# A decoder trunk on one Trainium2 core: a fourth Strassen unit in the last gate pair, earlier first splits, and another bank for the last group

## The chip, the cores and the metric

The kernel runs on one core of one Trainium2 chip. The metric is the device time of one execution in microseconds (us). Before the change it was 808.76 us, the median of 3 runs that lay between 808.56 and 809.57 us.

In the text PE is the matmul engine (TensorE), DVE the vector engine, ACT the scalar engine, POOL is GpSimd, and SP is the engine whose queue issues the DMAs. Each engine works through its own instructions strictly in the order in which the built program has them.

## The reference, cut to what matters

One layer on 256 tokens of width 2048, all in float32. The branches make a merge `m`, which is multiplied by `w_o`; then comes a gated per-layer embedding and a last norm:

```python
m = jax.nn.sigmoid(ga) * (ya @ w_a_out[i]) + jax.nn.sigmoid(gb) * (yb @ w_b_out[i])
x = x + m @ w_o[i]
gate = jax.nn.sigmoid(rmsnorm(x, ple_norm_g[i]) @ w_ple_gate[i])
x = x + gate * (p[i] @ w_ple_proj[i])
...
return rmsnorm(x, final_norm_g)
```

The change lies in the product with `w_ple_gate` (2048 x 2048, called `w_pg` in the kernel) and in what stands just before and behind it.

## The kernel before, in words

**Splits.** Every float32 product is made of three fp32r matmuls: weights and operands are split into a high part and a low remainder, and hi·hi, hi·lo and lo·hi are added up in PSUM. The weights arrive in raw tiles of 1 MB (tag `raw`, three buffers), which the SP queue loads. `split` (L143 and on) makes `whi` from a raw tile on ACT (L166) and `wlo` on DVE (L167), a [128, 1024] piece at a time; such a piece is one *position* of the plan. The three matmuls of one position for one 128-token half are recorded at L1265 (plain groups) or L1287 (pairs). The tokens are two halves, t = 0 and 1.

**The plan.** `groups` lists the products one after the other, each with 512 output columns or, for a pair, with 1024. The last ones are `OO` (a pair of `w_o`), two plain `w_o` groups, then for `w_pg`: the plain group PG 0 (columns 0 to 511), the pair GP (columns 512 to 1535, the program `LATE`), and the plain group PG 3 (columns 1536 to 2047), called the last group here. PG 0 has 8 positions of 12 matmuls.

**Pairs and Strassen units.** A pair is a list of units. A unit `(g, c)` takes two weight pieces of column half `g`; `(2, c)` takes the same piece `c` of both halves. Each has 2 splits and 24 matmuls. A unit `("S", c)` makes the piece `c` of both halves in Strassen's manner, in four positions: 21 matmuls and 4 splits (one of them half as wide), but DVE must first combine the weights in place (`combine_weights`, L181, L184, L185), and the operand has to be there in combined *forms* too (`forms`, tiles `So0`, `So1`). The sums 1, 5, 6 and 7 of the Strassen units gather in PSUM banks of tag `s`, those of the four outputs in banks of tag `g`; each tag has four banks. When the counts in `left` are at zero, `sums` adds the banks up on DVE (L852), after ACT has copied the first `s` bank (L865).

**The operand.** The operand of `w_pg` is the new `x`, turned. Each `w_o` group gives a quarter of it: `ep_o` adds it to `x`, sends it through DRAM (`turned`: four DMAs out, one back), DVE transposes blocks (L355), and `put` splits it with the norm's gain into `xh` on ACT (L310) and `xl` on DVE (L311). The last quarter (columns 1536 to 2047 of `x`) is read by positions 6 and 7 of PG 0. The third argument, 4 for that quarter, says how many steps later the transposition is recorded.

**The order.** The code records instructions in a loop over positions; `ahead(pos)` says how many positions ahead the splits are recorded, and rises from 3 to 8 in the course of the pair. A scheduler then decides how they stand on each engine, bound by data and by the few `issue_after` lines; what it made is seen in the built program only.

**The gates.** `gated` takes the sums of 512 columns: ACT the sigmoid (L1021), DVE the product with the projected embedding `pw` (L1024) and the sum into `xs` (L1025), ACT the squares (L1026), POOL the product with the last norm's gain (L1033). For the last group, `last_half` does the same in pieces of 256 columns (L1041, L1042, L1045, L1049). `sums_so_far` (L1058 to L1070) and `last_norm` (L1076, L1079) make the norm's factors, half of it on POOL; L1083, L1085 and L1087 scale `x`, and six DMAs write it out.

Of the kernel before, what the change touches and what calls it, by code (L numbers as in the profile page):

```python
# [12 lines left out]
ALU = mybir.AluOpType  # L13
PSUM = bass.MemoryType.PSUM

P = 128
# [7 lines left out]
CW = 512  # L24
# [19 lines left out]
INNER = (0, 4), ("S", 0), (0, 6), ("S", 1), (2, 3), ("S", 2), (1, 4), (1, 6)  # L44
FRONT = (0, 2), (0, 4), (0, 6), ("S", 0), (1, 2), ("S", 1), (1, 4), (1, 6)
OUT = (0, 4), ("S", 0), (1, 4), ("S", 1), (2, 3), ("S", 2), (0, 6), (1, 6)
LATE = (0, 4), ("S", 0), (0, 6), ("S", 1), (2, 3), ("S", 2), (1, 4), (1, 6)


PRM_GMIX, PRM_GPLE, PRM_GHG, PRM_LB, PRM_CONV = 0, 16, 32, 40, 48  # L50
# [5 lines left out]
def hybrid_kernel(ctx, tc, xT, x, pT, prm, gfin, masks, w_in, w_a, w_b, w_o, w_pg, w_pp, out):  # L56
    nc = tc.nc
# [23 lines left out]
    state = {"tmp": "tmp1"}  # L81
# [3 lines left out]
    def nm(s):  # L85
        uid[0] += 1
        return f"{s}_{uid[0]}"

    def t4(tag="t4", bufs=None):
        bufs = bufs or {"tmp1": 8, "tmp2": 4, "tmp3": 5}[state["tmp"]]  # L90
        return pools[state["tmp"]].tile([P, 1024], F32, tag=tag, bufs=bufs, name=nm(tag))

    def bank(tag):
        return ps.tile([P, CW], F32, tag=tag, bufs=4, name=nm(tag))

    def sc(n, tag="sc", bufs=12):
        return small.tile([P, n], F32, tag=tag, bufs=bufs, name=nm(tag))
# [9 lines left out]
    def load(pos):  # L107
        if unit_of[pos] not in loaded and groups[steps[pos][0]][0] == "O":
            with tc.issue_after(state["sent"]):
                return load_raw(pos)  # L110
        return load_raw(pos)
# [62 lines left out]
    def combine_weights(pos):  # L174

        b = load(pos).rearrange("p i (k c) -> p (i k) c", k=2)
        pool, tag, n = ("tmp2", "t2", 2) if more(pos) in ("gates", "last") else ("tmp3", "t2", 1)
        if more(pos) in ("inner", "first"):
            pool, tag, n = "tmp1", ("both", "aoff")[unit_of[pos] // 2 % 2], 1
        t2 = half[unit_of[pos]] = pools[pool].tile([P, CW], F32, tag=tag, bufs=n, name=nm("t2"))  # L180
        nc.vector.tensor_tensor(  # L181
            out=b[:, 0:4:3, :], in0=b[:, 0:3:2, :], in1=b[:, 3:4, :].to_broadcast([P, 2, CW]), op=ALU.subtract
        )
        nc.vector.tensor_tensor(out=t2, in0=b[:, 2, :], in1=b[:, 0, :], op=ALU.add)  # L184
        nc.vector.tensor_tensor(out=b[:, 1, :], in0=b[:, 1, :], in1=t2, op=ALU.subtract)  # L185

# [14 lines left out]
    groups += [("OO", 0, w_o, 0, "mT", OUT), ("O", 2, w_o, 2, "mT"), ("O", 3, w_o, 3, "mT")]  # L201
    groups += [("PG", 0, w_pg, 0, "x1T"), ("GP", 1, w_pg, 1, "x1T", LATE), ("PG", 3, w_pg, 3, "x1T")]
    steps = []
# [25 lines left out]
    LEAD = 3  # L229
# [10 lines left out]
    gates, late = of_kind("GG"), of_kind("PG")[0]  # L240
# [18 lines left out]
    def more(pos):  # L259

        return "gates" if pos in gates else "last" if pos in last else "outer" if pos in outer else "first" if pos in g0 else "inner" if any(pos in at for at in inner) else None
# [24 lines left out]
    def gain(base, k):  # L286
        return prm_t[:, base + k : base + k + 1]
# [15 lines left out]
    def put(op, k, src, scale=None):  # L303

        hi, lo = op[0][:, k, :], op[1][:, k, :]
        if scale is None:
            nc.scalar.activation(out=hi, in_=src, func=AF.Copy)
            nc.vector.tensor_tensor(out=lo, in0=src, in1=hi.bitcast(F32), op=ALU.subtract)
        else:
            a = nc.scalar.activation(out=hi, in_=src, func=AF.Identity, scale=scale)  # L310
            v = nc.vector.scalar_tensor_tensor(  # L311
                out=lo, in0=src, scalar=scale, in1=hi.bitcast(F32), op0=ALU.mult, op1=ALU.subtract
            )
            return a.ins, v.ins
# [12 lines left out]
    def blocks(ap):  # L327

        return ap.rearrange("p (c b e) -> p c b e", b=4, e=32)

    def spread(ap, t):

        return ap.rearrange("p (b c t e) -> p t c b e", b=4, c=4, t=NT)[:, t]

    def turned(src, lag, dst=None):

        d = dram.tile([P, 4, T], F32, tag="turn", bufs=3, name=nm("turn"))
        to = d.rearrange("(b i) a x -> a i b x", b=4)
        for a in range(4):
            state["sent"] = nc.sync.dma_start(
                out=to[a], in_=src[32 * a : 32 * a + 32, :].rearrange("i (b x) -> i b x", b=4)
            ).ins
        yield  # L350
        nc.sync.dma_start(out=src, in_=d.rearrange("p a x -> p (a x)"))
        for _ in range(lag):
            yield
        dst = t4() if dst is None else dst
        nc.vector.transpose(  # L355
            out=dst.rearrange("p (k a e) -> p a k e", a=4, e=32), in_=src.rearrange("p (a k e) -> p a k e", a=4, e=32)
        )
        return dst
# [439 lines left out]
    def form_tiles(pool, tag, n=2):  # L798

        return lambda: tuple(pool.tile([P, 4 * n * P], F32R, tag=tag + x, bufs=1, name=nm(tag + x)) for x in "hl")  # L800
# [50 lines left out]
    def add(out, x, y):  # L851
        nc.vector.tensor_tensor(out=out, in0=x, in1=y, op=ALU.add)  # L852
# [95 lines left out]
    def ep_o(j, psum):  # L948
        xs = state["x"]
        x1 = t4()  # L950
        for t in range(NT):
            d = xs[:, t, j * CW : (j + 1) * CW]
            add(d, d, psum[t])
            nc.scalar.activation(out=spread(x1, t), in_=blocks(d), func=AF.Copy)
        turn = turned(x1, (2, 6, 6, 4)[j])
        next(turn)
        yield
        junk = t4()
        next(turn)
        for t in range(NT):  # L960
            nc.scalar.activation(
                out=junk[:, t * CW : (t + 1) * CW], in_=xs[:, t, j * CW : (j + 1) * CW], func=AF.Square,
                accum_out=state["ss2"][:, t * 4 + j : t * 4 + j + 1],
            )
        yield
        x1 = yield from turn
        if j < 2:
            for c in range(4):
                h = x1[:, c * T : (c + 1) * T]
                nc.scalar.activation(out=h, in_=h, func=AF.Identity, scale=gain(PRM_GPLE, j * 4 + c))  # L970
            hi, lo = (x[:, j * 4 : j * 4 + 4, :].rearrange("p k t -> p (k t)") for x in state["x1T"])
            nc.scalar.activation(out=hi, in_=x1, func=AF.Copy)
            nc.vector.tensor_tensor(out=lo, in0=x1, in1=hi.bitcast(F32), op=ALU.subtract)
            yield
            chunks = [c for u, c in LATE if u == "S" and c // 2 == j]
            r = x1.rearrange("p (u k t) -> p u k t", u=2, k=2)[:, : len(chunks)]
            yield from forms("x1T", form_tiles(pools["tmp3"], f"So{j}", len(chunks)), r, chunks)
            return
        for c in range(4):
            state["splits"] = put(state["x1T"], j * 4 + c, x1[:, c * T : (c + 1) * T], gain(PRM_GPLE, j * 4 + c))  # L980
        if j == 3:
            tot = sc(2, "tot2", 1)
            nc.vector.tensor_reduce(
                out=tot, in_=state["ss2"].rearrange("p (t j) -> p t j", t=NT),
                axis=mybir.AxisListType.X, op=ALU.add,
            )
            state["rstd2"] = rsqrt_of(tot, NT, D, "r2")
# [257 lines left out]
    def advance():  # L1245
        for e in list(active):
            step(e)
# [5 lines left out]
    def ahead(pos):  # L1253

        at, n = more(pos + LEAD), 0
        while n < len(MORE[at]) and more(pos + LEAD + n + 1) == at and (at == "gates" or more(pos + LEAD - 2 * n) == at):
            n += 1
        return LEAD + min(max(pos - late - 4, 0) // 3, 5) + n

    def product(psum, op, k, t, hi, lo, first, last, which=(0, 1, 2)):  # L1260

# [64 lines left out]
    for pos, (gi, c) in enumerate(steps[:last_group]):  # L1326
# [7 lines left out]
        order = ExitStack()  # L1334
# [77 lines left out]
        for i in range(2):  # L1412
            k = 2 * c + i
            for c0, c1 in EARLY[0][:2] if pos == 0 and i == 0 else ((0, CW),):
                s = slice(i * CW + c0, i * CW + c1)
# [35 lines left out]

    nlast = len(steps) - last_group
    for t, halves in ((0, (0, 1)), (1, (0,)), (1, (1,))):
        bk, n = bank("g"), CW // 2
        for c in range(nlast):
            if done < len(steps):
                split(done)
                done += 1
            hi, lo = parts[last_group + c]
            for i in range(2):  # L1460
                k = 2 * c + i
                s = slice(i * CW + halves[0] * n, i * CW + (halves[-1] + 1) * n)
                product(bk[:, : len(halves) * n], state["x1T"], k, t, hi[:, s], lo[:, s], k == 0, k == KT - 1)
            if c % 2:
                advance()
        if t == 0:
            active.append(ep_last(t, [bk[:, h * n : (h + 1) * n] for h in halves]))
        else:
            last_half(t, halves[0], bk[:, :n])
            if halves[0] == 0:  # L1470
                sums_so_far(t)
# [76 lines left out]
```

## Time and profile before

| what | value |
|---|---|
| time, median of 3 runs | 808.76 us (808.56 to 809.57) |
| profiled execution, its own time | 808.2 us |
| its span, first to last instruction | 806.4 us |
| PE busy | 797.0 us, 99% of the span |
| DVE busy | 685.2 us, 85% |
| ACT busy | 494.3 us, 61% |
| POOL busy | 94.5 us, 12% |
| mean granted PE clock | 0.998 |

The span is 1.8 us shorter than the time of the same execution. All positions in time below are in us from the span's start. In a row of the timeline stand the start, how long it took, the engine and the line, what is written and read with its shape, how many instructions of that kind follow each other ("x2"), and in brackets how long the engine had been idle before it and what released it. Tiles have their buffer numbers left out there: `t` is any of the work tiles, `g` and `s` are PSUM banks.

### The profile page before, as it was taken

What the parts mean: (1) busy time and instruction counts of PE and PEld (TensorE: products, weight loads), DVE (VectorE), ACT (ScalarE), POOL (GpSimd) and SP (SyncE); (2) the same over time, 40 slices, a digit from 0 to 9 for tenths busy, and PEclk for the clock granted to TensorE, in tenths of its full rate; (3) what the DMA queues carried; (4) which work ended last, traced back from release to release, by engine and by line L of the source; (5) the groups of instructions that cost most, each with busy time, mean ns of one, the idle gap of its engine ahead of it and who ended that gap; (6) DMA issues with size and microseconds to landing.
All of it is one profiled execution on the core that took longest, in us unless ns stands there. A gap on an engine that the chain in (4) does not pass through costs nothing. (4 is left out here: it accounts for less than half of the span.)

```text
span 806.4 us, 11109 instructions
## 1 busy us (share of the span) xinstructions
PE 797.0 (99%) x4168; PEld 662.0 (82%) x4169; DVE 685.2 (85%) x794; ACT 494.3 (61%) x666; POOL 94.5 (12%) x74
## 2 busy tenths in 40 slices
PE   9999999999999999999999999999999999999995
PEld 7888888888888888888888888888888888888785
DVE  5969797966778987978998998998998988859995
ACT  7867565575665755586674564564565557746562
POOL 0000145300000044300001001000100000002032
PEclk9999999999999999999999999999999999999999
DMA  9898855747676755667584775775875679985542
GB/s 340 309 335 313 269 175 206 234 165 240 242 262 208 259 172 196 213 217 250 189 306 158 234 274 170 235 265 179 280 267 192 207 247 360 327 299 207 201 178 104
DMA packets 50309, 191.20 MB, mean 237 GB/s; under 512 B 5712, under 2 KB 15184, under 8 KB 36304
## 3 DMA queue, kind: packets, MB, share of 16 engines
q1 hardware_dynamic: 50112, 190.24, 68.6%
q8 instruction: 32, 0.52, 0.3%
q10 hardware_dynamic: 144, 0.26, 0.1%
q14 instruction: 21, 0.17, 0.1%
HBM read 175.80 MB, written 14.68 MB: 236 GB/s over the span
## 5 line engine op out<-in xcount | busy, mean ns | idle before, releaser
L167 DVE TENSOR_TENSOR wlo<-raw,whi 128x1024 fp32r<-128x1024 f32 (+1 forms) x320 | 391.1, 1246 | 83.6 <-ACT whi L166 82.1
L166 ACT ACTIVATE whi<-raw 128x1024 fp32r<-128x1024 f32 (+1 forms) x320 | 326.2, 1047 | 163.9 <-PE g L1265 93.5
L1265 PE MATMUL g<-whi,xh 128*128 128x512 f32 (+1 forms) x464 | 177.4, 383 | 0.0
L1265 PE MATMUL g<-whi,xl 128*128 128x512 f32 (+1 forms) x464 | 177.2, 382 | 0.0
L1265 PE MATMUL g<-wlo,xh 128*128 128x512 f32 (+1 forms) x464 | 177.1, 382 | 0.0
L1287 PE MATMUL g<-wlo,xh 128*128 128x512 f32 x316 | 122.9, 389 | 0.0
L1287 PE MATMUL g<-whi,xl 128*128 128x512 f32 x316 | 122.9, 389 | 0.0
L1287 PE MATMUL g<-whi,xh 128*128 128x512 f32 x316 | 122.4, 389 | 0.0
L1265 PEld LDWEIGHTS g<-whi,xl 128*128 128x128 f32 x464 | 87.2, 188 | 17.0
L1265 PEld LDWEIGHTS g<-wlo,xh 128*128 128x128 f32 x464 | 87.2, 188 | 16.7
L1265 PEld LDWEIGHTS g<-whi,xh 128*128 128x128 f32 x464 | 87.2, 188 | 16.7
L166 ACT ACTIVATE whi<-t 128x512 fp32r<-128x512 f32 x25 | 15.8, 632 | 90.8 <-DVE t L184 90.8
L1287 PEld LDWEIGHTS g<-whi,xl 128*128 128x128 f32 x316 | 59.3, 188 | 12.4
L1287 PEld LDWEIGHTS g<-wlo,xh 128*128 128x128 f32 x316 | 59.3, 188 | 12.3
L1287 PEld LDWEIGHTS g<-whi,xh 128*128 128x128 f32 x316 | 59.3, 188 | 12.2
L934 POOL TENSOR_TENSOR t<-ga,gb 128x512 f32<-128x512 f32 x6 | 10.6, 1793 | 188.0 <-issue 118.1
L181 DVE TENSOR_TENSOR raw<-raw 128x1024 f32<-128x1024 f32 x25 | 31.6, 1263 | 0.7
L1265 PE MATMUL g<-whi,yaTh 128*128 128x512 f32 (+1 forms) x74 | 28.0, 385 | 0.0
L1265 PE MATMUL g<-wlo,yaTh 128*128 128x512 f32 (+1 forms) x74 | 27.9, 383 | 0.0
L1265 PE MATMUL g<-whi,yaTl 128*128 128x512 f32 (+1 forms) x74 | 27.9, 383 | 0.0
L1265 PE MATMUL g<-whi,ybTh 128*128 128x512 f32 x64 | 24.9, 389 | 0.0
L1265 PE MATMUL g<-wlo,ybTh 128*128 128x512 f32 x64 | 24.9, 389 | 0.0
(317 smaller groups left out, 1114.9 us busy)
## 6 DMA issues: line engine op xcount, KB each, us to landing
raw<-in_w_in SPq DMA_DIRECT2D x68, 1024.0 KB, 4.9
raw<-in_w_in SPq DMA_DIRECT2D x37, 512.0 KB, 5.1
raw<-in_w_o SPq DMA_DIRECT2D x12, 1024.0 KB, 5.9
raw<-in_w_pg SPq DMA_DIRECT2D x12, 1024.0 KB, 5.6
raw<-in_w_in SPq DMA_DIRECT2D x38, 256.0 KB, 5.1
turn<-t SPq DMA_DIRECT2D x72, 128.0 KB, 2.8
t<-turn SPq DMA_DIRECT2D x18, 512.0 KB, 4.9
raw<-in_w_a SPq DMA_DIRECT2D x8, 1024.0 KB, 5.4
```

Of the source, the lines that this page charges most:

```text
L166: a = nc.scalar.activation(out=hi[:, s], in_=src[:, s], func=AF.Copy)
L167: v = nc.vector.tensor_tensor(out=lo[:, s], in0=src[:, s], in1=hi[:, s].bitcast(F32), op=ALU.subtract)
L181: nc.vector.tensor_tensor(out=b[:, 0:4:3, :], in0=b[:, 0:3:2, :], in1=b[:, 3:4, :].to_broadcast([P, 2, CW]), op=ALU.subtract)
L934: (nc.vector if j == 3 else nc.gpsimd).tensor_tensor(out=spread(m, t), in0=blocks(ga[:, s]), in1=blocks(gb[:, s]), op=ALU.add)
L1265: nc.tensor.matmul(psum, a, b, start=first and n == 0, stop=last and n == 2)
L1287: nc.tensor.matmul(banks[name], x, y[:, s], start=k == total[name] and i == 0, stop=k == 1 and i == 2)
```

## The change

It has five edits. In `LATE`, the unit `(2, 3)` and one place of order give way to `("S", 3)`, so that four of the eight units are Strassen units, the last of them just ahead of the final plain unit. The forms of the second quarter are made for two pieces in place of one (that follows from `LATE`). `ahead` reaches its depth two positions sooner. The last quarter's transposition is recorded one step later (5 for 4), and the combination of the weights of the first Strassen unit after it has to stand behind the last `put`. The last group's first accumulation takes a bank of tag `s` in place of `g`.

```diff
-LATE = (0, 4), ("S", 0), (0, 6), ("S", 1), (2, 3), ("S", 2), (1, 4), (1, 6)
+LATE = (0, 4), ("S", 0), (0, 6), ("S", 1), (1, 4), ("S", 2), ("S", 3), (1, 6)
...
-        nc.vector.tensor_tensor(
-            out=b[:, 0:4:3, :], in0=b[:, 0:3:2, :], in1=b[:, 3:4, :].to_broadcast([P, 2, CW]), op=ALU.subtract
-        )
+        with ExitStack() as order:
+            for i in state.pop("puts", ()):
+                order.enter_context(tc.issue_after(i))
+            nc.vector.tensor_tensor(
+                out=b[:, 0:4:3, :], in0=b[:, 0:3:2, :], in1=b[:, 3:4, :].to_broadcast([P, 2, CW]), op=ALU.subtract
+            )
...
-        turn = turned(x1, (2, 6, 6, 4)[j])
+        turn = turned(x1, (2, 6, 6, 5)[j])
...
         if j == 3:
+            state["puts"] = state["splits"]
...
-        return LEAD + min(max(pos - late - 4, 0) // 3, 5) + n
+        return LEAD + min(max(pos - late - 2, 0) // 3, 5) + n
...
-        bk, n = bank("g"), CW // 2
+        bk, n = bank("g" if t else "s"), CW // 2
```

The changed file has up to four lines more, so its line numbers are higher by 3 or 4: L355 becomes L358, L1024 becomes L1028, L1265 becomes L1269, L1287 becomes L1291. What the scheduler made of it is shown at three places.

**DVE, around the last quarter's transposition.** Before, from the last split of PG 0 to the first gates (`wlo_1137` and `wlo_1140` are the splits of the pair's first unit, `wlo_1142` the first of its first Strassen unit):

```order
L167 TENSOR_TENSOR wlo_1130_6365<-raw_1113_6271,whi_1129_6364 128x1024
L983 TENSOR_REDUCE tot2_1132_6390<-ss2_1036_5822 128x2
L320 TENSOR_SCALAR r2v_1133_6392<-tot2_1132_6390 128x2
L355 STREAM_TRANSPOSE t4_1131_6380<-t4_1114_6273 128x4x8x32
L311 SCALAR_TENSOR_TENSOR xl_1039_5826<-t4_1131_6380,prm_t_84,xh_1038_5825 128x256 x4
L167 TENSOR_TENSOR wlo_1137_6399<-raw_1123_6326,whi_1136_6398 128x1024
L167 TENSOR_TENSOR wlo_1140_6417<-raw_1123_6326,whi_1139_6416 128x1024
L167 TENSOR_TENSOR wlo_1142_6433<-raw_1128_6360,whi_1141_6432 128x1024
L181 TENSOR_TENSOR raw_1128_6360<-raw_1128_6360 128x2x512
```

Now, from the same split on (`wlo_1133`, `wlo_1135` and `wlo_1142` are the same three):

```order
L167 TENSOR_TENSOR wlo_1130_6365<-raw_1113_6271,whi_1129_6364 128x1024
L167 TENSOR_TENSOR wlo_1133_6383<-raw_1123_6326,whi_1132_6382 128x1024
L167 TENSOR_TENSOR wlo_1135_6387<-raw_1123_6326,whi_1134_6386 128x1024
L987 TENSOR_REDUCE tot2_1138_6414<-ss2_1036_5822 128x2
L323 TENSOR_SCALAR r2v_1139_6416<-tot2_1138_6414 128x2
L167 TENSOR_TENSOR wlo_1142_6421<-raw_1128_6360,whi_1141_6420 128x1024
L358 STREAM_TRANSPOSE t4_1137_6404<-t4_1114_6273 128x4x8x32
L314 SCALAR_TENSOR_TENSOR xl_1039_5826<-t4_1137_6404,prm_t_84,xh_1038_5825 128x256 x4
L184 TENSOR_TENSOR raw_1128_6360<-raw_1128_6360 128x2x512
```

The three splits moved ahead of the transposition. Six rows further, the remaining split of that Strassen unit (`wlo_1150`) now stands ahead of the first gates (L1028), where before it stood behind them (L1024, L1025). The splits of the next unit stand behind the gates in both, on DVE (`wlo_1156`) as on ACT (`whi_1155`, behind the two sigmoids of L1021, now L1025).

**PE, at the seam of PG 0 and the pair.** `g_1118` and `g_1119` are the two banks of PG 0, `g_1151` to `g_1154` banks of the pair. Before, PG 0's position 6 (`whi_1126`) follows its position 5 (`whi_1124`):

```order
L1265 MATMUL g_1119_6293<-whi_1124_6328,xh_1038_5825 128x512
L1265 MATMUL g_1119_6293<-wlo_1125_6329,xh_1038_5825 128x512
L1265 MATMUL g_1119_6293<-whi_1124_6328,xl_1039_5826 128x512
L1265 MATMUL g_1118_6292<-whi_1126_6344,xh_1038_5825 128x512
L1265 MATMUL g_1118_6292<-wlo_1127_6345,xh_1038_5825 128x512
L1265 MATMUL g_1118_6292<-whi_1126_6344,xl_1039_5826 128x512
```

Now the pair's first unit stands behind position 5:

```order
L1269 MATMUL g_1119_6293<-whi_1124_6328,xh_1038_5825 128x512
L1269 MATMUL g_1119_6293<-wlo_1125_6329,xh_1038_5825 128x512
L1269 MATMUL g_1119_6293<-whi_1124_6328,xl_1039_5826 128x512
L1291 MATMUL g_1153_6478<-whi_1132_6382,xh_1038_5825 128x512
L1291 MATMUL g_1153_6478<-wlo_1133_6383,xh_1038_5825 128x512
L1291 MATMUL g_1153_6478<-whi_1132_6382,xl_1039_5826 128x512
```

and PG 0's position 6 comes 30 matmuls later, behind the first position of the Strassen unit:

```order
L1291 MATMUL g_1153_6478<-whi_1141_6420,xh_1038_5825 128x512
L1291 MATMUL s_1160_6516<-wlo_1142_6421,xh_1038_5825 128x512
L1291 MATMUL s_1160_6516<-whi_1141_6420,xl_1039_5826 128x512
L1291 MATMUL g_1153_6478<-wlo_1142_6421,xh_1038_5825 128x512
L1291 MATMUL g_1153_6478<-whi_1141_6420,xl_1039_5826 128x512
L1269 MATMUL g_1118_6292<-whi_1126_6344,xh_1038_5825 128x512
L1269 MATMUL g_1118_6292<-wlo_1127_6345,xh_1038_5825 128x512
```

So 30 matmuls of the pair (24 of the unit `(0, 4)` and 6 of the Strassen unit) moved ahead of the last 24 of PG 0.

**DVE, at the end.** Before, the first 128 tokens' sums are finished and scaled (L1085, L1087) ahead of the next piece (`t4_1232`):

```order
L1058 TENSOR_TENSOR ss3_1037_5823<-ss3_1037_5823 128x1
L1062 TENSOR_REDUCE tot3_1229_6899<-ss3_1037_5823 128x1
L1076 TENSOR_TENSOR tot3_1229_6899<-tot3_1229_6899,ss3_1037_5823 128x1
L1085 TENSOR_SCALAR xs_5814<-xs_5814,r3_1231_6907 128x256 x2
L1087 SCALAR_TENSOR_TENSOR xs_5814<-xs_5814,r3_1231_6907,gfin_t_6044 128x512
L1042 TENSOR_TENSOR t4_1232_6954<-t4_1232_6954,pw_1218_6767 128x256
```

Now the next piece (`t4_1237`) stands among those sums:

```order
L1062 TENSOR_TENSOR ss3_1037_5823<-ss3_1037_5823 128x1
L1046 TENSOR_TENSOR t4_1237_6964<-t4_1237_6964,pw_1227_6809 128x256
L1066 TENSOR_REDUCE tot3_1234_6909<-ss3_1037_5823 128x1
L1049 TENSOR_TENSOR xs_5814<-xs_5814,t4_1237_6964 128x256
L1080 TENSOR_TENSOR tot3_1234_6909<-tot3_1234_6909,ss3_1037_5823 128x1
L1053 SCALAR_TENSOR_TENSOR t4_1237_6964,ss3_1037_5823<-xs_5814 128x256
L1089 TENSOR_SCALAR xs_5814<-xs_5814,r3_1236_6917 128x256 x2
L1091 SCALAR_TENSOR_TENSOR xs_5814<-xs_5814,r3_1236_6917,gfin_t_6044 128x512
```

Three instructions of 256 columns moved ahead of the first half's scaling.

## The prediction

> **What bounds the kernel now.** First the page's busy times, then the waits of PE.
>
> ```profile
> PE 797.0 (99%) x4168; PEld 662.0 (82%) x4169; DVE 685.2 (85%) x794; ACT 494.3 (61%) x666; POOL 94.5 (12%) x74
> PE s L1287 <- DVE wlo L167: 0.2, 1, 0.2
> ```
>
> PE is busy nearly all the time, and the view of its waits names one late wait. The starts of matmuls in PE's timeline show more (the pair runs from 733.21, the last group from 775.78, its first piece of 256 columns from 786.66):
>
> ```profile
> 733.21 0.39 PE L1287 MATMUL g<-whi,xh 128*128 128x512 f32 x1
> 740.69 0.39 PE L1287 MATMUL s<-whi,So0h 128*128 128x512 f32 x1
> 741.14 0.50 PE L1287 MATMUL s<-wlo,So0h 128*128 128x512 f32 x1
> 751.52 0.40 PE L1287 MATMUL s<-whi,So0h 128*128 128x512 f32 x1
> 752.08 0.50 PE L1287 MATMUL s<-wlo,So0h 128*128 128x512 f32 x1 [0.17 <-DVE wlo L167]
> 775.78 0.39 PE L1265 MATMUL g<-whi,xh 128*128 128x512 f32 x1
> 786.66 0.28 PE L1265 MATMUL g<-whi,xh 128*128 128x256 f32 x1
> 798.05 0.28 PE L1265 MATMUL g<-whi,xl 128*128 128x256 f32 x1
> ```
>
> From 775.78 to 786.66 stand 48 matmuls: one per 0.2267 us, whatever a row says of its length. The pair has 5 x 24 + 3 x 21 = 183, which is 41.48 us, but takes 42.57. So PE loses 1.09 us there, at the first two Strassen units, each time for a `wlo`: in this stretch DVE hands over just in time. DVE's timeline there, with the first gates (L1024, L1025) in the middle:
>
> ```profile
> 720.11 0.17 DVE L320 TENSOR_SCALAR r2v<-tot 128x2 f32<-128x2 f32 x1
> 725.61 1.25 DVE L355 STREAM_TRANSPOSE t<-t 128x1024 f32<-128x1024 f32 x1 [5.34 <-DMA t<-turn]
> 729.59 3.50 DVE L167 TENSOR_TENSOR wlo<-raw,whi 128x1024 fp32r<-128x1024 f32 x3 [0.47 <-ACT whi L166]
> 737.46 1.29 DVE L1024 TENSOR_TENSOR t<-t,pw 128x512 f32<-128x512 f32 x2
> 738.66 1.29 DVE L1025 TENSOR_TENSOR xs<-xs,t 128x512 f32<-128x512 f32 x2
> 739.87 4.62 DVE L167 TENSOR_TENSOR wlo<-raw,whi 128x1024 fp32r<-128x1024 f32 x4
> 744.52 2.20 DVE L181 TENSOR_TENSOR raw<-raw 128x1024 f32<-128x1024 f32 x1
> 746.76 1.67 DVE L184 TENSOR_TENSOR t<-raw 128x512 f32<-128x512 f32 x1
> 755.47 1.23 DVE L181 TENSOR_TENSOR raw<-raw 128x1024 f32<-128x1024 f32 x1
> 756.73 0.69 DVE L184 TENSOR_TENSOR t<-raw 128x512 f32<-128x512 f32 x1
> 757.45 0.69 DVE L185 TENSOR_TENSOR raw<-raw,t 128x512 f32<-128x512 f32 x1
> 758.18 0.69 DVE L167 TENSOR_TENSOR wlo<-t,whi 128x512 fp32r<-128x512 f32 x1
> 759.35 6.90 DVE L167 TENSOR_TENSOR wlo<-raw,whi 128x1024 fp32r<-128x1024 f32 x6 [0.48 <-ACT whi L166]
> 767.70 2.36 DVE L167 TENSOR_TENSOR wlo<-raw,whi 128x1024 fp32r<-128x1024 f32 x2 [1.45 <-ACT whi L166]
> ```
>
> The reader is to see that DVE is idle for 5.34 us while the last quarter of `x` comes back from DRAM, and then has hardly a gap until 766.2.
>
> **The change part by part.**
>
> *The three splits.* They fill 3.50 us of those 5.34 us. That alone is worth little: what comes next on DVE decides.
>
> *The seam on PE.* Thirty matmuls of the pair now stand ahead of PG 0's last 24, so PG 0 ends 30 x 0.2267 = 6.80 us later: at 740.01 in place of 733.21. The first gates take PG 0's two banks, whose last matmuls stand fourth from the end and at the end: starts at 739.10 and 739.78. How soon ACT follows is shown by the last piece:
>
> ```profile
> 735.99 1.25 ACT L1021 ACTIVATE t<-g,r2r 128x512 f32<-128x512 f32 x2
> 798.37 0.47 ACT L1041 ACTIVATE t<-g,r2r 128x256 f32<-128x256 f32 x1 [3.19 <-PE g L1265]
> ```
>
> 798.37 - 798.05 = 0.32, and a sigmoid takes some 0.63. So the second one ends at 739.78 + 0.32 + 0.63 = 740.73, where before both were done at 737.24. DVE's second product starts then (0.6), the two sums follow (1.2), and the next split (`wlo_1156`) starts at 742.5. Before, it was the second of the four from 739.87, at 741.0. **DVE resumes 1.5 us later.** All that it can do ahead (puts until 729.1, a combination of 2.7 and splits of 2.9) is done at 734.7, so it idles 5 to 6 us ahead of the gates: the old gap is moved, not closed. On ACT the splits `whi_1155` and on, on DVE all further splits, are queued behind those gates, and PE waits for them.
>
> *The fourth unit.* On PE it saves 3 x 0.2267 = 0.68 us. On DVE the combination takes 758.18 - 755.47 = 2.71, three splits 3 x 6.90/6 = 3.45, the half one 0.6, together 6.8 against 2.3 for the two splits of a plain unit: **4.5 us more**. The idle time of 1.45 us at 767.70 (a raw tile's load) lies behind the third Strassen unit before and should lie behind the fourth now; I count it once in both, between 0 and another 1.45.
>
> *POOL.* L181 took 2.20 and L184 1.67 at 744.52, against 1.23 and 0.69 at 755.47. In that stretch POOL multiplied for the first gates:
>
> ```profile
> 740.82 7.06 POOL L1033 TENSOR_TENSOR xs<-xs,gfin_t 128x512 f32<-128x512 f32 x2 [19.76 <-ACT t L1026]
> 788.00 2.73 POOL L1033 TENSOR_TENSOR xs<-xs,gfin_t 128x512 f32<-128x512 f32 x2 [2.59 <-ACT t L1026]
> ```
>
> The gates and the next combination move together, so I leave the two hits of 0.97 where they are; at best they vanish (-1.95).
>
> *The second quarter's forms* for two pieces: four operations grow from 128 to 256 columns and one remainder from 512 to 1024, by the rows of such splits (0.69 and 1.15) 0.5 us and by the columns about 0.5 us more. DVE has room behind it:
>
> ```profile
> 710.08 1.22 DVE L167 TENSOR_TENSOR wlo<-raw,whi 128x1024 fp32r<-128x1024 f32 x1 [1.72 <-ACT whi L166]
> ```
>
> That covers 1.0; uncovered, it would push PG 0's splits, which PE needs only 5 us later. It costs nothing. So do the later `pw` loads on SP's queue (their readers come later still) and the new `issue_after` (the combination stands behind the puts on DVE anyway).
>
> *The end.* DVE is 1.5 + 4.5 = 6.0 us late when it finishes the last pair's gates. What follows before:
>
> ```profile
> 786.48 1.28 DVE L1025 TENSOR_TENSOR xs<-xs,t 128x512 f32<-128x512 f32 x2
> 788.93 2.08 DVE L1042 TENSOR_TENSOR t<-t,pw 128x256 f32<-128x256 f32 x2 [1.17 <-ACT t L1041]
> 790.93 0.75 DVE L1045 TENSOR_TENSOR xs<-xs,t 128x256 f32<-128x256 f32 x2
> 792.29 0.15 DVE L1058 TENSOR_TENSOR ss<-ss 128x1 f32<-128x1 f32 x1
> 792.66 0.16 DVE L1076 TENSOR_TENSOR tot<-tot,ss 128x1 f32<-128x1 f32 x1
> 793.49 0.61 DVE L1085 TENSOR_SCALAR xs<-xs,r 128x256 f32<-128x256 f32 x2 [0.66 <-POOL r L1079]
> 794.02 0.74 DVE L1087 SCALAR_TENSOR_TENSOR xs<-xs,r,gfin_t 128x512 f32<-128x512 f32 x1
> 795.22 0.42 DVE L1042 TENSOR_TENSOR t<-t,pw 128x256 f32<-128x256 f32 x1 [0.45 <-ACT t L1041]
> 796.60 0.16 DVE L1058 TENSOR_TENSOR ss<-ss 128x1 f32<-128x1 f32 x1
> 797.87 0.16 DVE L1070 TENSOR_TENSOR xs<-tot,tot 128x1 f32<-128x1 f32 x1 [0.73 <-POOL tot L1069]
> 798.88 0.43 DVE L1042 TENSOR_TENSOR t<-t,pw 128x256 f32<-128x256 f32 x1 [0.85 <-ACT t L1041]
> ```
>
> Gates done at 787.76 + 6.0 = 793.8; the first sums 792.29 - 787.76 = 4.5 later, at 798.3; five instructions in the new order (0.15, 0.33, 0.17, 0.33, 0.16) until 799.4; POOL and back 0.67, 800.1; scaling 1.27, 801.4; the second sums with their POOL step 1.43, 802.8. There the last piece's product starts, at 798.88 before: **3.9 us later**. The lateness of 6.0 has lost 2.1 in gaps that were waits for PE or ACT, and in the piece that stands among the sums. From here on to the output nothing changes.
>
> *PE beside it.* It must be done by 802.8 - 0.83 = 802.0. From 798.05 it loses 0.68, gains 1.5 at the second Strassen unit (it waited for DVE there already), and 0 to 2 at the fourth and where the last group waits for its `s` bank (ACT copies that sum behind late splits): 798.9 to 800.9. So PE is no longer what ends the kernel, and those waits cost nothing more.
>
> **Sum.** 806.4 + 3.9 = 810.3 us of span. The profiled execution took 808.2, 0.56 under the median; the same difference put on the median gives 808.76 + 3.9 = **812.7 us**.
>
> **The rivals.**
>
> *Faster: the splits pay for the unit.* Were the first gates not held by the seam, DVE would be 3.5 us ahead from the transposition on, and only 1.0 behind at the last group, where waits of 1.17, 0.45 and 0.85 absorb it; PE's 1.09 us of waits would go with the 0.68: 808.76 - 1.77 = 807.0. It decides from the point where `wlo_1156` starts: at 741.0 or earlier. For it speaks the gap of 5.34 us; against it the order on PE, which is fixed. 5%.
>
> *Only the matmuls count.* PE has 99% of the span and DVE slack elsewhere: 808.76 - 0.68 = 808.1. Against it: PE's losses at 741.14 and 752.08 are DVE's. 5%. The Trainium skill, in "Perfetto Trace Analysis", section Identifying Performance Opportunities, says that improving a kernel generally means improving its most-contended engine; by that rule this result would come. The rows of the pair's stretch speak against it.
>
> *POOL's hits miss.* If the products with the gain fall into the new gap or behind the combination, DVE gets 1.95 back: 812.7 - 1.95 = 810.7. For it: POOL's two took 2.73 at 788.00, with DVE idle. Against: they follow the squares, which follow DVE's sums, so they cannot fall into the gap. 13%.
>
> *More waits.* A raw tile late once more (1.45), or PE past 802.0: 814.2 to 814.8. 11%.
>
> **How the numbers follow.** Forecast 66%, with half a microsecond to either side for the resumption and 0.5 for the unit's price: 811.7 to 813.7. The range takes in the two neighbours: 810.4 to 814.8, and leaves out the first two rivals. Within 0.2% (1.6 us, about what a measurement of this kernel can tell from no change) lie the second rival and a third of POOL's: 9%. Faster by more: 5%. Slower by more: 86%.
>
> **What would show it.** In the changed profile DVE's wait ahead of L358 is under 2 us, and a wait of 5 to 6 us for ACT's L1025 stands ahead of L1028, at about 740. PE's L1269 rows of PG 0 end at 740. L184 and L187 of the second Strassen unit are long again. PE waits for `whi` or `wlo` there and at the fourth unit. The last matmul starts at 799 to 801, and the last L1046 over 1 us after the sigmoid ahead of it. Wrong it would be if `wlo_1156` starts before 741, or if DVE has gaps of more than 2 us behind the fourth unit.

## The result, and the profile after

The changed kernel takes **812.60 us** (median of 7 runs, 812.32 to 813.28) against 808.76 before, 3.84 us more. The ratio estimated from the runs of both is 1.0041, with a 95% interval from 1.0030 to 1.0053: slower. (That of the two medians is 1.0047. The seven runs of the kernel before beside it have the same median, 808.76, and lie between 808.27 and 811.78.) The profiled execution took 812.58 us, with a span of 810.8 us, 4.4 us above the one before.

The busy times of the page have hardly moved, and could not have told it:

```profile
PE 797.4 (98%) x4165; PEld 661.0 (82%) x4166; DVE 690.5 (85%) x799; ACT 495.7 (61%) x668; POOL 88.9 (11%) x74
```

PE has three matmuls fewer, DVE 5.3 us more. The seam is seen in PE's timeline. The last matmul of PG 0's position 5 starts at 727.65 and the pair's first unit follows; PG 0's last matmul starts at 739.89 (732.99 before):

```profile
727.65 0.39 PE L1269 MATMUL g<-whi,xl 128*128 128x512 f32 x1
727.88 0.39 PE L1291 MATMUL g<-whi,xh 128*128 128x512 f32 x1
...
739.89 0.39 PE L1269 MATMUL g<-whi,xl 128*128 128x512 f32 x1
740.12 0.62 PE L1291 MATMUL s<-whi,So0h 128*128 128x512 f32 x2
...
751.39 0.51 PE L1291 MATMUL s<-whi,So0h 128*128 128x512 f32 x1 [0.86 <-ACT whi L166]
752.34 0.50 PE L1291 MATMUL s<-whi,So0h 128*128 128x512 f32 x1 [0.45 <-ACT whi L166]
...
777.98 0.50 PE L1269 MATMUL s<-whi,xh 128*128 128x512 f32 x1 [0.70 <-ACT t L868]
...
800.42 0.28 PE L1269 MATMUL g<-whi,xl 128*128 128x256 f32 x1
```

The same on DVE, from the transposition to the end. The brackets are to be read one after the other: the gap ahead of L358 has shrunk from 5.34 to 0.55, and a new one of 5.25 stands ahead of the first gates. The old gap isn't wholly gone: 1.55 us of it now stand ahead of the third split, whose `whi` comes after a raw tile's load.

```profile
724.41 1.23 DVE L167 TENSOR_TENSOR wlo<-raw,whi 128x1024 fp32r<-128x1024 f32 x1 [1.55 <-ACT whi L166]
726.19 1.25 DVE L358 STREAM_TRANSPOSE t<-t 128x1024 f32<-128x1024 f32 x1 [0.55 <-DMA t<-turn]
...
740.41 1.33 DVE L1028 TENSOR_TENSOR t<-t,pw 128x512 f32<-128x512 f32 x2 [5.25 <-ACT t L1025]
741.65 1.29 DVE L1029 TENSOR_TENSOR xs<-xs,t 128x512 f32<-128x512 f32 x2
742.86 4.58 DVE L167 TENSOR_TENSOR wlo<-raw,whi 128x1024 fp32r<-128x1024 f32 x3
747.47 2.20 DVE L184 TENSOR_TENSOR raw<-raw 128x1024 f32<-128x1024 f32 x1
749.71 0.69 DVE L187 TENSOR_TENSOR t<-raw 128x512 f32<-128x512 f32 x1
...
776.52 2.36 DVE L167 TENSOR_TENSOR wlo<-raw,whi 128x1024 fp32r<-128x1024 f32 x2 [1.58 <-ACT whi L166]
...
793.14 1.28 DVE L1029 TENSOR_TENSOR xs<-xs,t 128x512 f32<-128x512 f32 x2
795.58 2.08 DVE L1046 TENSOR_TENSOR t<-t,pw 128x256 f32<-128x256 f32 x2 [1.17 <-ACT t L1045]
...
803.25 0.16 DVE L1074 TENSOR_TENSOR xs<-tot,tot 128x1 f32<-128x1 f32 x1 [0.73 <-POOL tot L1073]
803.33 0.42 DVE L1046 TENSOR_TENSOR t<-t,pw 128x256 f32<-128x256 f32 x1
```

DVE is 742.86 - 741.0 = 1.9 us late behind the first gates, 794.42 - 787.76 = 6.7 us late behind the last pair's, and 803.33 - 798.88 = 4.45 us late at the last product. That last row has no bracket: its sigmoid on ACT was done at 802.03 + 0.45 = 802.48, so DVE and not PE ends the kernel.

```profile
802.03 0.45 ACT L1045 ACTIVATE t<-g,r2r 128x256 f32<-128x256 f32 x1
```

### The profile page after: what moved, and what is told of

It reads as the page before. It is cut to its first block, busy times and chain, and to the rows that moved or that the text cites. A ratio compares the mean times of both kernels' runs of the same rounds, so it can differ in the third digit from the quotient of the medians.

```text
span 810.8 us, 11121 instructions
## 1 busy us (share of the span) xinstructions
PE 797.4 (98%) x4165; PEld 661.0 (82%) x4166; DVE 690.5 (85%) x799; ACT 495.7 (61%) x668; POOL 88.9 (11%) x74
## 4 chain that ended last, share of the span: by engine, by line
PE 90%; DVE 5%; issue 2%; ACT 1%; DMA 1%; POOL 0%; ACTq 0%; POOLq 0%; DVEq 0%
PE g L1269 48%; PE g L1291 29%; PE s L1291 7%; PE s L1269 3%; DVE wlo L167 2%; DMA raw<-in_w_pg 1%; PE s L514 1%; DVE raw L184 1%; DVE t L1028 1%; PE s L1142 1%; DVE xs L1029 0%; DVE t L855 0%; DVE t L1046 0%; ACT whi L166 0%; DVE t L187 0%
## 5 line engine op out<-in xcount | busy, mean ns | idle before, releaser
L1269 PE MATMUL g<-whi,xh 128*128 128x512 f32 (+1 forms) x448 | 171.2, 383 | 0.0
L1269 PE MATMUL g<-wlo,xh 128*128 128x512 f32 (+1 forms) x448 | 170.9, 382 | 0.0
L1269 PE MATMUL g<-whi,xl 128*128 128x512 f32 (+1 forms) x448 | 170.9, 382 | 0.0
L1291 PE MATMUL g<-wlo,xh 128*128 128x512 f32 x310 | 120.6, 389 | 0.0
L1291 PE MATMUL g<-whi,xl 128*128 128x512 f32 x310 | 120.6, 389 | 0.0
L1291 PE MATMUL g<-whi,xh 128*128 128x512 f32 x310 | 120.0, 389 | 0.0
L1269 PEld LDWEIGHTS g<-whi,xl 128*128 128x128 f32 x448 | 84.2, 188 | 16.4
L1269 PEld LDWEIGHTS g<-whi,xh 128*128 128x128 f32 x448 | 84.2, 188 | 16.2
L1269 PEld LDWEIGHTS g<-wlo,xh 128*128 128x128 f32 x448 | 84.2, 188 | 16.1
L1291 PEld LDWEIGHTS g<-whi,xl 128*128 128x128 f32 x310 | 58.2, 188 | 12.1
L1291 PEld LDWEIGHTS g<-wlo,xh 128*128 128x128 f32 x310 | 58.2, 188 | 12.0
L1291 PEld LDWEIGHTS g<-whi,xh 128*128 128x128 f32 x310 | 58.2, 188 | 12.0
L184 DVE TENSOR_TENSOR raw<-raw 128x1024 f32<-128x1024 f32 x26 | 32.8, 1261 | 0.7
L1269 PE MATMUL g<-whi,yaTh 128*128 128x512 f32 (+1 forms) x74 | 28.0, 385 | 0.0
L1269 PE MATMUL g<-wlo,yaTh 128*128 128x512 f32 (+1 forms) x74 | 27.9, 384 | 0.0
L1269 PE MATMUL g<-whi,yaTl 128*128 128x512 f32 (+1 forms) x74 | 27.9, 383 | 0.0
L1269 PE MATMUL g<-whi,ybTh 128*128 128x512 f32 x64 | 24.9, 389 | 0.0
L1269 PE MATMUL g<-wlo,ybTh 128*128 128x512 f32 x64 | 24.9, 389 | 0.0
```

The source lines that it names most:

```text
L184: nc.vector.tensor_tensor(out=b[:, 0:4:3, :], in0=b[:, 0:3:2, :], in1=b[:, 3:4, :].to_broadcast([P, 2, CW]), op=ALU.subtract)
L1269: nc.tensor.matmul(psum, a, b, start=first and n == 0, stop=last and n == 2)
L1291: nc.tensor.matmul(banks[name], x, y[:, s], start=k == total[name] and i == 0, stop=k == 1 and i == 2)
```

## The experiments

The theory to be tried: the 3.84 us are DVE's lateness at the end, made of the resumption behind the first gates (which the seam on PE holds back) and of the fourth unit's work, less what the tail absorbs. The rivals: the unit alone does it; the moves alone; the bank; POOL.

| kernel | seam on PE | Strassen units | median us | ratio to before, 95% |
|---|---|---|---|---|
| changed | 30 matmuls between | 4 | 812.60 | 1.0041 (1.0030 to 1.0053) |
| e1_unit | as before | 4 | 811.78 | 1.0038 (1.0024 to 1.0052) |
| e2_moves | 30 between | 3 | 810.03 | 1.0014 (1.0003 to 1.0025) |
| e3_bank | 30 between | 4 | 813.90 | 1.0059 (1.0046 to 1.0072) |
| e4_seam | 3 between | 4 | 808.89 | 0.9995 (0.9987 to 1.0004) |
| e5_three | 3 between | 3 | 807.48 | 0.9971 (0.9962 to 0.9980) |
| e6_nopool | 30 between | 4 | 810.85 | 1.0023 (1.0014 to 1.0032) |
| e7_tail | 3 between | 4 | 807.11 | 0.9973 (0.9962 to 0.9984) |
| e8_twelve | 12 between | 4 | 809.47 | 0.9997 (0.9988 to 1.0006) |

The kernel before stood at 809.1 to 809.3 in the runs beside these. They were taken in three groups (e1 to e4, e5 to e7, e8) apart from the changed kernel's, so kernels of different groups are better compared by their ratios than by their medians. In e1, e2 and e3 the last group begins in a bank of tag `g`, in the others in one of tag `s`.

**e1_unit: the fourth unit alone.** The kernel before with one line changed:

```diff
-LATE = (0, 4), ("S", 0), (0, 6), ("S", 1), (2, 3), ("S", 2), (1, 4), (1, 6)
+LATE = (0, 4), ("S", 0), (0, 6), ("S", 1), (1, 4), ("S", 2), ("S", 3), (1, 6)
```

> The kernel before with the changed program LATE alone (and the forms that follow from it); the seam on PE, the transposition, `ahead` and the last group's bank stay as before. Seam theory (the change's 3.9 us are made of 1.5 to 1.9 us by which DVE resumes late behind the first gates and 4.5 us of DVE work of the fourth unit, less some 2.1 us that the tail absorbs): the first gates stay at 736 to 740, the split behind them at 741.0; only the 4.5 us are left, so + 2.4 us, 811.2 (810.5 to 812.0). Rival 'the unit alone': the moves are worth nothing and the unit's DVE work does it all: + 3.8, 812.6. Rival 'the moves alone': the unit fits into DVE's slack and PE saves 0.68 us: 808.1.

Measured: 811.78, 2.7 us above the 809.12 beside it. The rival "the moves alone" (808.1) falls: the unit costs. "The unit alone" forecast 3.8 us more, a ratio of about 1.0047, which lies inside this run's interval, so this run does not exclude it; e4_seam below, with four units and no loss, does. The profiled execution of this kernel took 813.8, 2 us above its median (the sums of the last quarter of `x`, L852 on DVE, start at 712.63 against 711.22 before, and the transposition at 727.27), so its end is not compared. Its waits show where PE pays, at the new unit, for a `wlo`:

```profile
769.01 0.50 PE L1287 MATMUL s<-wlo,So1h 128*128 128x512 f32 x1 [0.70 <-DVE wlo L167]
770.14 0.50 PE L1287 MATMUL s<-wlo,So1h 128*128 128x512 f32 x1 [0.16 <-DVE wlo L167]
```

**e2_moves: all but the unit and the bank.** The changed kernel with these two edits:

```diff
-LATE = (0, 4), ("S", 0), (0, 6), ("S", 1), (1, 4), ("S", 2), ("S", 3), (1, 6)
+LATE = (0, 4), ("S", 0), (0, 6), ("S", 1), (2, 3), ("S", 2), (1, 4), (1, 6)
...
-        bk, n = bank("g" if t else "s"), CW // 2
+        bk, n = bank("g"), CW // 2
```

> The changed kernel with the program LATE of before and the last group in a bank of tag g: the moves alone (splits ahead of the transposition, 30 matmuls of the pair between PG 0's, `ahead` two positions sooner). Seam theory: DVE resumes 1.5 to 1.9 us late, as in the changed kernel, and idles 5 us ahead of the first gates. PE's two losses at the first two Strassen units (1.09 us before) become the 1.7 us or so that the changed kernel's starts show at 751.39 and 752.34, and the tail's slack of 2.1 takes up DVE's lateness: + 0.8 us, 809.6 (808.9 to 810.6). Rival 'the unit alone': no difference, 808.8. Rival 'the moves alone': the whole + 3.8, 812.6. Rival 'the moves gain' (a gap of 5.34 us is filled with 3.5 us of work): - 1.1 us, 807.7.

Measured: 810.03, 0.9 us above the 809.12 beside it. The gap of DVE has moved as in the changed kernel, and the splits behind it start at the same time:

```profile
726.70 1.25 DVE L358 STREAM_TRANSPOSE t<-t 128x1024 f32<-128x1024 f32 x1 [0.92 <-DMA t<-turn]
...
740.45 1.32 DVE L1028 TENSOR_TENSOR t<-t,pw 128x512 f32<-128x512 f32 x2 [4.78 <-ACT t L1025]
741.69 1.29 DVE L1029 TENSOR_TENSOR xs<-xs,t 128x512 f32<-128x512 f32 x2
742.89 4.59 DVE L167 TENSOR_TENSOR wlo<-raw,whi 128x1024 fp32r<-128x1024 f32 x3
```

So the resumption is late without the fourth unit too, but alone it costs little. That three units leave DVE room to catch up is argued, not shown here. (This profiled execution too took 2.2 us more than the median of its kernel; nothing is read from its end.)

**e3_bank: the last group in a bank of tag `g` again.** The changed kernel with

```diff
-        bk, n = bank("g" if t else "s"), CW // 2
+        bk, n = bank("g"), CW // 2
```

> The changed kernel with the last group's first accumulation in a bank of tag g again. Seam theory: DVE ends the kernel, not PE, so the bank is worth nothing at the end although PE waits otherwise at the group's start (0 to 1.5 us more, since the g bank has to be read out by the last pair's sums): within 0.3 us of the changed kernel, 812.3 to 812.9; PE has room of 1.6 us (802.0 less 800.42). Rival 'the bank': the wait of 1.09 us for the copied s bank at 776.88 is part of the loss: 811.5. Rival 'the bank gains': PE's start would be later than its room allows, over 813.4.

Measured: 813.90, 1.3 us above the changed kernel. The expectation was wrong: I had given PE a room of 1.6 us, and it needed more. PE now waits until DVE's sums (L855) have read the bank out, and its first matmul of the last group starts at 779.78 in place of 777.98. The next ones come 0.43 us apart in place of 0.227:

```profile
777.14 0.39 PE L1291 MATMUL g<-whi,xl 128*128 128x512 f32 x1
779.78 0.79 PE L1269 MATMUL g<-whi,xh 128*128 128x512 f32 x1 [2.26 <-DVE t L855]
780.38 0.63 PE L1269 MATMUL g<-wlo,xh 128*128 128x512 f32 x1
780.80 0.63 PE L1269 MATMUL g<-whi,xl 128*128 128x512 f32 x1
...
783.29 0.39 PE L1269 MATMUL g<-whi,xl 128*128 128x512 f32 x1
```

In this stretch, 779.7 to 783.4, the profile has a granted PE clock of 0.54, and 1.00 on either side; in the changed kernel, behind a wait of 0.70, it is 1.00 throughout. So the bank costs PE twice: 1.8 us by the later start and 1.6 us by the slow pace behind the wait. Its last matmul starts at 803.79 against 800.42, 3.4 us later, which is more than the room. The last product on DVE then waits for PE's sums by way of the sigmoid, 804.62 - 803.33 = 1.29 us later than in the changed kernel:

```profile
804.62 0.43 DVE L1046 TENSOR_TENSOR t<-t,pw 128x256 f32<-128x256 f32 x1 [1.05 <-ACT t L1045]
```

So the bank of tag `s` is an edit that gains in the changed kernel: it keeps PE from being later at the end than DVE is.

**e4_seam: PG 0 held together on PE.** The changed kernel with an order for the pair's first unit; `state["mm"]` is the last matmul recorded so far, which is PG 0's last:

```diff
-            nc.tensor.matmul(psum, a, b, start=first and n == 0, stop=last and n == 2)
+            state["mm"] = nc.tensor.matmul(psum, a, b, start=first and n == 0, stop=last and n == 2).ins
...
-            pair_products(c, program, opname)
+            with ExitStack() as seam:
+                if kind == "GP" and c[0] == 0:
+                    seam.enter_context(tc.issue_after(state["mm"]))
+                pair_products(c, program, opname)
```

> The changed kernel with one line more of order: the pair's first matmul may not be issued ahead of PG 0's last, so PG 0 is held together on PE as before, while the three splits stay ahead of the transposition on DVE. Seam theory: the first gates come back to 733 to 737, and DVE is 3.5 us ahead there: the fourth unit's 4.5 us are paid but for 1.0 us, PE's 1.09 us of waits go with the 0.68 us of matmuls; PE's last matmul 1.5 us earlier than before. The tail's changed order (a piece among the first half's sums) gives about 0.9 us back: 808.2 (807.0 to 809.2), 4.4 us under the changed kernel. Rival 'the unit alone': the seam is worth nothing or at most its 1.5 us: 811.1 to 812.6. Rival 'PE waits at the transposition': with no foreign matmuls, PE stands still while the last quarter comes back, and the gain is lost there: 811 or more, with a wait ahead of PG 0's position 6.

Measured: 808.89, 3.7 us under the changed kernel by this one order, and 0.2 us under the 809.12 beside it, a difference that its interval does not tell from none. The order holds back the unit `(0, 4)`; three matmuls of the first Strassen unit still stand between PG 0's. DVE's rows, to be held against those of the changed kernel:

```profile
725.19 1.23 DVE L167 TENSOR_TENSOR wlo<-raw,whi 128x1024 fp32r<-128x1024 f32 x1 [2.58 <-ACT whi L166]
726.42 1.25 DVE L358 STREAM_TRANSPOSE t<-t 128x1024 f32<-128x1024 f32 x1
...
735.30 1.29 DVE L1028 TENSOR_TENSOR t<-t,pw 128x512 f32<-128x512 f32 x2
736.51 1.29 DVE L1029 TENSOR_TENSOR xs<-xs,t 128x512 f32<-128x512 f32 x2
737.71 3.49 DVE L167 TENSOR_TENSOR wlo<-raw,whi 128x1024 fp32r<-128x1024 f32 x3
...
787.74 1.28 DVE L1029 TENSOR_TENSOR xs<-xs,t 128x512 f32<-128x512 f32 x2
...
799.23 0.42 DVE L1046 TENSOR_TENSOR t<-t,pw 128x256 f32<-128x256 f32 x1
```

There is no gap right ahead of L358 or of L1028 any more (2.58 us of waiting for a `whi` stand one row earlier), and the split behind the gates starts at 737.71, 5.15 us earlier than in the changed kernel and 3.3 earlier than before. The view of PE's waits is empty from 700 on. So the seam is a cause: this one order takes the loss away with the unit still there. It is not the only one, since the unit cost 2.7 us in e1_unit, where PG 0 was whole. What pays for the unit here are the splits done ahead, and with the seam broken those had gained nothing (e2_moves). (One side effect: at the end this kernel's DVE scales the first half ahead of the next piece, as before the change. From the end of the last pair's gates to the last product it takes 10.21 us, the changed kernel 8.91, so this is no part of the gain.)

**e5_three: the same with three units.** e4_seam with `LATE` as before:

```diff
-LATE = (0, 4), ("S", 0), (0, 6), ("S", 1), (1, 4), ("S", 2), ("S", 3), (1, 6)
+LATE = (0, 4), ("S", 0), (0, 6), ("S", 1), (2, 3), ("S", 2), (1, 4), (1, 6)
```

> The kernel with PG 0 held together on PE (as in the run before this), but with three Strassen units, the program LATE of before. Seam theory: with the gates at their old place and three splits done ahead, DVE is 3.5 us ahead, PE's two waits (1.09 us) go, and since the last pair's gates are early, PE's last matmul ends the kernel again: 808.76 - 1.1 = 807.7 (807.2 to 808.3), 2.3 us under the same moves without the seam's line. Rival 'the splits gain nothing': 808.8. Rival 'PE waits elsewhere' (a raw tile's load becomes late when DVE and ACT hand on sooner): 808.3 to 809.5, with a wait of PE behind 760.

Measured: 807.48, faster than before (1.7 us under the 809.21 beside it). PE has no wait from 700 on, and ends the kernel again: DVE waits 2.87 us for the last sigmoid.

```profile
798.73 0.42 DVE L1046 TENSOR_TENSOR t<-t,pw 128x256 f32<-128x256 f32 x1 [2.87 <-ACT t L1045]
```

Against e2_moves, which has three units too, it is 2.5 us less, by the seam's order and the last group's bank together.

So the fourth unit costs 808.89 - 807.48 = 1.4 us here, 2.7 us in e1_unit and 813.90 - 810.03 = 3.9 us between e2_moves and e3_bank; by the ratios 1.9, 3.1 and 3.6, each with an interval of 1.0 to 1.4 us to either side. That fits "the later DVE already is, the more", but intervals this wide do not prove the order.

**e6_nopool: POOL's two products left out.** In `gated` of the changed kernel:

```diff
-        for t in range(NT):
+        for t in range(NT if j else 0):
             d = xs[:, t, j * CW : (j + 1) * CW]
             nc.gpsimd.tensor_tensor(out=d, in0=d, in1=state["gfin"][:, j * CW : (j + 1) * CW], op=ALU.mult)
```

> The changed kernel with the two products of the first gates with the last norm's gain left out on POOL (512 columns of the output stay without the gain). Theory 'two hits on the path': the split from 742.86 (4.58 for three, 3.5 elsewhere) and L184 at 747.47 (2.20, 1.23 elsewhere) get their 2.05 us back, PE's waits at the second Strassen unit (1.0 and 0.7) go with them, and as DVE's lateness of 6.66 falls to 4.6 all of it comes out at the end: - 1.8 us of the changed kernel's 812.6, 810.8 (810.4 to 811.4). Rival 'hidden': DVE has gaps behind it (1.58 for a raw tile, 1.17 and 0.73 in the tail) that take it up: 812.0 to 812.6. Rival 'not POOL' (the long rows have another cause, as a wait that moved): the rows stay long, 812.6.

Measured: 810.85, 1.75 us under the changed kernel (1.5 by the ratios). The long rows are short again:

```profile
742.58 3.49 DVE L167 TENSOR_TENSOR wlo<-raw,whi 128x1024 fp32r<-128x1024 f32 x3
746.11 1.23 DVE L184 TENSOR_TENSOR raw<-raw 128x1024 f32<-128x1024 f32 x1
```

So POOL's two products delay DVE by 4.58 - 3.49 and 2.20 - 1.23, 2.06 us in all, and 1.75 of it reach the end. They are not new with the change: the kernel before has two such delays, 1.95 us in all. What leaving POOL's products out would give there was not run. The Trainium skill, in "SBUF — State Buffer", section Who interferes with whom, says that a DVE instruction with two SBUF inputs contends with a GpSimd instruction that reads SBUF; the two rows of this run and the two of the changed kernel agree.

**e7_tail: another order at the end.** e4_seam with the last group's third piece recorded ahead of both halves' sums, and the first half's scaling behind the second half's sum:

```diff
         last_half(t, 0, halves[0])
-        sums_so_far(t)
         last_half(t, 1, halves[1])
-        last_norm(t)
         yield
...
+        if t == 0:
+            sums_so_far(1)
+            order.enter_context(tc.issue_after(state["piece"]))
...
             if halves[0] == 0:
-                sums_so_far(t)
+                with tc.issue_after(state["piece"]):
+                    sums_so_far(0)
+                    last_norm(0)
```

`state["piece"]` is the last instruction on DVE of the piece, and then of the second half's sum; `order` is closed at the end of `last_norm`.

> The kernel with PG 0 held together on PE and four units, and another order at the end: the last group's third piece (second half of the tokens, first 256 columns) ahead of both halves' sums, then both powers on POOL, and the first half's scaling behind them. Theory 'DVE's tail is what ends that kernel' (PE's last matmul starts at 796.38, but the last product on DVE at 799.23, 2.0 us later than PE would need): about 1 us is saved until PE ends it again, 0.32 + 0.6 behind the last matmul, so 797.4 to 798.2 for the last product: 807.6 (807.2 to 808.2), under every kernel so far but perhaps the one with three units. Rival 'the tail is bound by POOL and the sigmoids': no gain, 808.9. Rival 'slower': the first half's output leaves about 1.5 us later and its DMAs collide with the second half's: 809.5.

Measured: 807.11, 2.1 us under the 809.21 beside it and just under the range expected. From the end of the last pair's gates (789.12) to the last product it is 8.73 us, where e4_seam takes 799.23 - 789.02 = 10.21:

```profile
787.84 1.28 DVE L1029 TENSOR_TENSOR xs<-xs,t 128x512 f32<-128x512 f32 x2
...
797.85 0.43 DVE L1046 TENSOR_TENSOR t<-t,pw 128x256 f32<-128x256 f32 x1
```

It beats both kernels, as e5_three does; the two can't be told apart by their intervals. So the fourth unit, even paid for, has gained nothing that shows; three units with this order at the end were not run.

**e8_twelve: twelve matmuls between.** e4_seam with the order put on all but the pair's first position:

```diff
-                if kind == "GP" and c[0] == 0:
+                if kind == "GP" and c[0] < 2 and c != (0, 0):
```

> Four units, and 12 matmuls of the pair (its first position) ahead of PG 0's last 24, in place of the 3 of the run with PG 0 held together and the 30 of the changed kernel; all else as in those two. Seam theory with a threshold: the first gates come 9 x 0.2267 = 2.0 us later than with PG 0 held together, but until about 736.4 DVE has a split more to do ahead of them, so that it idles 0.5 us only and resumes 0.6 us later: 808.9 + 0.5 = 809.4 (808.8 to 809.9). Rival 'in proportion' (each foreign matmul costs the same, 3.7 us over 27): 808.9 + 1.2 = 810.1. Rival 'any break of PG 0 costs' (the mixing itself, not the wait): 812 or more.

Measured: 809.47, as expected, by its ratio 0.2 us above e4_seam (0.6 by the medians). Two splits stand right ahead of the gates, where e4_seam has one; the gates start 1.75 us later than there, with no gap:

```profile
734.77 2.35 DVE L167 TENSOR_TENSOR wlo<-raw,whi 128x1024 fp32r<-128x1024 f32 x2
737.05 1.32 DVE L1028 TENSOR_TENSOR t<-t,pw 128x512 f32<-128x512 f32 x2
738.29 1.29 DVE L1029 TENSOR_TENSOR xs<-xs,t 128x512 f32<-128x512 f32 x2
```

That a broken PG 0 costs as such (812 or more) is ruled out. "In proportion" (1.2 us above e4_seam) is less likely than a threshold, but the intervals don't exclude it.

## Why the prediction was right

- **The seam.** PG 0's last matmul was put at 739.78 and starts at 739.89. The gap "moved, not closed": 5.25 us ahead of L1028, forecast 5 to 6. e4_seam shows that the seam makes it.
- **The resumption.** Forecast 1.5 us late, measured 1.9: the first sigmoid starts at 739.69 (739.42 by the forecast), and the two end at 741.01 and not 740.73:

```profile
739.69 1.32 ACT L1025 ACTIVATE t<-g,r2r 128x512 f32<-128x512 f32 x2 [6.16 <-issue]
```

- **The unit.** Forecast 4.5 us of DVE; from 1.9 late to 6.7 late are 4.8. The raw tile's gap came once, 1.58 us (1.45 before), as counted.
- **POOL.** Two hits of 0.97 were kept where they were. There were two (1.09 and 0.97), but the first fell on a split ahead of L184, and L187 took its usual 0.69, so "L184 and L187 long again" is half right. The rival's price for both, 1.95 us, was 1.75 in e6_nopool.
- **The tail.** Forecast to absorb 2.1 us, measured 6.66 - 4.45 = 2.2. The last product was put 3.9 us later and came 4.45 later in this execution; the median is up by 3.84. That 812.7 and 812.60 agree to 0.1 us is luck: the resumption and the unit were put 0.4 and 0.3 us too small, and the two profiled executions differ by 4.4 us, but the one before lay 0.56 us under its median and the one after at its own. The sign that it would stand "over 1 us after the sigmoid" came out as 803.33 against 802.48, 0.85 us from the sigmoid's end (1.30 from its start).
- **PE.** Its last matmul starts at 800.42, inside the forecast 798.9 to 800.9. The step held, but through an edit that I priced at nothing: with the `g` bank PE ends the kernel, 1.3 us later still (e3_bank). The sum was right since it was made for the changed bank; what the bank is worth it did not see.
- **The rival "faster".** It said 807.0 if the seam did not hold the gates. e4_seam, which is that case, took 808.89. Its last matmul on PE did come 1.67 us earlier (796.38 against 798.05), but DVE ended the kernel: the last pair's gates end at 789.02, 1.3 late, and the last product starts at 799.23, 0.35 later than before (798.88), where the rival's sum had it 1.77 earlier. With the order at the end changed, the number came: 807.11 (e7_tail).
- **The rule of the most-contended engine**, which the prediction cited from the Trainium skill ("Perfetto Trace Analysis", section Identifying Performance Opportunities), gave 808.1 with PE taken as that engine by its matmul time, 99% of the span. Here PE lost three matmuls, and the kernel grew slower by 3.84 us. (By its weight loads, PEld in the profile before, the same engine was at 82%, below DVE's 85%.)

What set the seam is seen in two more built programs, which were not run: with the third argument of `turned` at 4 and all else as changed, no matmul of the pair stands between PG 0's; with 5 and the old `ahead`, 12 do. So the 30 come from two numbers together, of which the first is the one that lets the pair in.

## What to carry to other kernels

A gap that one edit fills on an engine is a gain only if what comes next on that engine is ready earlier too: look up who feeds the next instruction, and whether the same edit has pushed that work back in its own queue. Trading matmuls for vector work can pay only where the vector engine has room at that place: the fourth unit cost 1.4 to 3.9 us for 0.68 us of matmuls. When an engine's lateness reaches the tail, the order of the tail decides how much of it is seen (10.21 or 8.73 us for the same work).

## What had not been expected of the hardware

A POOL product that meets DVE's rows costs about the same wherever it falls (1.09 us on a split, 0.97 on a combination), but which instruction it hits changes with small shifts: two rows of the combination before (L181 and L184), a split and the combination's first row after (L184 there).

A wait on PE can cost more than its own length. In e3_bank a wait of 2.26 us was followed by 3.5 us in which matmuls came 0.43 us apart, at a granted clock of 0.54, which cost another 1.6 us. Behind the waits of 0.70 us (changed kernel) and 1.17 us (e2_moves) the pace was 0.227 us again after one matmul. Where between 1.17 and 2.26 us that begins, no run here shows.

DVE's transposition of the last quarter started between 725.61 (before) and 727.27 (e1_unit). The greater part of this is not the way through DRAM: the sums that feed it (L852) started at 711.22 and 712.63, so from there to the transposition it was 14.39 and 14.64 us. In e2_moves it was 15.34 (711.36 to 726.70).
